# Token projections, gates and branch products of a hybrid attention block: fp16 halves scaled by powers of two in place of fp32r halves

## The chip, the cores and the metric

The kernel runs on one core of a Trainium2 chip. A core has a matrix engine (PE, with its weight loads shown apart as PEld), a vector engine (DVE), a scalar engine (ACT), a general engine (POOL) and a queue that issues DMAs (SP). Matmuls write to PSUM, an accumulator memory in banks of 512 fp32 columns; everything else lies in SBUF, 128 partitions wide. The metric is the device time of one execution in microseconds, the median of several runs.

## The reference

One decoder layer over 528 tokens (16 learned meta tokens and 512 real ones) with a model width of 1024. Two attention branches of 16 heads each, MLA and a forgetting attention (FoX), run on the same normalized input `u`; one projection `w_in` gives all branch inputs and gates:

```python
u = rmsnorm(h, pre_norm_g[l])
proj = u @ w_in[l]
(cq, ckv, k_pe_raw, z_mla, fq, fk, fv, f_logit, z_fox, gate_a, gate_b) = jnp.split(proj, split_idx, axis=-1)
...
y_mla = (o_mla * jax.nn.silu(z_mla)) @ w_br_mla[l]
...
y_fox = (o_fox * jax.nn.silu(z_fox)) @ w_br_fox[l]
mixed = (jax.nn.sigmoid(gate_a) * y_mla + jax.nn.sigmoid(gate_b) * y_fox) @ w_out[l]
h = h + rmsnorm(mixed, post_norm_g[l])
```

`o_mla` and `o_fox` are causal softmax attention; FoX adds a cumulative log forget gate to its logits. All inputs are fp32.

## The kernel before, in words

Every large product is made from halves. An fp32 operand is written as `hi + lo`, where `hi` is the operand rounded to the matmul's type and `lo` the remainder, and three matmuls `hi*hi`, `hi*lo`, `lo*hi` are added in PSUM (function `unit`, lines 161 to 184). Before the change the type is fp32r everywhere but for the attention probabilities and values, which are fp16 already.

**Front** (lines 247 to 398). `front(t)` normalizes one of five token tiles (four of 128, one of 16 meta tokens), transposes it by PE into PSUM (`pt`) and writes both halves of `u` into `uTh` and `uTl`. `back(t)` makes the small projections (`psm`: the latents, the rotary key, the forget logits) from them. The queries and keys of the first FoX head pair are projected in between, and the first forget-gate sums are made.

**Attention** (lines 413 to 740). Sixteen stages: for each of 8 head pairs first FoX (`br` 1), then MLA (`br` 0). Here the order of the PE work is written out by hand. A stage issues scores (`st`), the values of the stage before (`ov`), more scores, and then a list of filling steps (`fill`): the projections that the next stage needs and the two `z` gates of the pair. A FoX stage is filled with `z` of both branches, `mq`, `mk` and the MLA `v`; an MLA stage with `fq`, `fk` and the FoX `v`. One step is three matmuls for one of the `nk` blocks of 128 rows; a unit has 8 such blocks (512 columns) or 16 (272 and then 256 columns). The softmax runs as DVE mask and minimum (line 620), ACT exponential (628), ACT and DVE making the two halves of the probabilities (655, 656), POOL the part of the meta tokens (642 to 647) and DMA transposes issued from SP (661).

**Weights.** `wload` (94) issues the DMA of a weight block of 128 x 1024 fp32 into a ring of three buffers (`wraw`); `wsplit` (112) makes its halves: a cast on ACT (line 116) and a subtraction on POOL (line 117, recorded at the helper's line 92), in rings of three. `ahead` (692) makes each unit, when it starts, issue the loads of the next three. Other engines' orders come from a planner that goes by program order, with some parts raised.

**Merge** (lines 743 to 778). The 16 blocks of the gated branch outputs `gT` are split into `gh` and `gl` (ACT line 752, DVE line 753). For each of 8 blocks of 128 output columns there are two branch products `py` (FoX first), their gated sum `tb`, its halves `mh` and `ml`, and, for the first six, two gate units (`pg`). The last product (`po`, lines 781 to 840) and the second norm follow.

Unit outputs accumulate in a ring of three PSUM banks (`acc`, 156). All matmuls go through the helper at line 86, all transposes through the one at line 89, and all low halves made by a subtraction through the one at line 92; the profile shows these lines, and the tile names tell them apart.

Of the kernel before, what the change touches and what calls it, by code (L numbers as in the profile page):

```python
# [22 lines left out]
D = 1024  # L23
# [31 lines left out]
def block_kernel(ctx: ExitStack, tc: tile.TileContext, x, meta_tokens, pre_norm_g, w_in, fox_forget_b,  # L55
# [19 lines left out]
    uTh, uTl = (const.tile([128, KD, ROW + L - META], F32R, tag=n, name=n)[:, :, ROW - META :] for n in ("uTh", "uTl"))  # L75
# [6 lines left out]
    wp = ctx.enter_context(tc.tile_pool(name="wp", bufs=3))  # L82
    uid = [0]

# [9 lines left out]
    def wload(srcs):  # L94
# [3 lines left out]
        raw = wp.tile([128, 1024], F32, tag="wraw", name=f"wraw{u}")  # L98
# [13 lines left out]
    def wsplit(ld, keep=None):  # L112

        u, raw, parts, n = ld
        wh, wl = ((keep or wp).tile([128, 1024], F32R, tag=t, name=f"{t}{u}") for t in ("wh", "wl"))
        nc.scalar.copy(wh[:, :n], raw[:, :n])  # L116
        split_lo(nc.gpsimd, wl[:, :n], raw[:, :n], wh[:, :n])
        return [(wh[:, o : o + w], wl[:, o : o + w]) for o, w in parts]

    def wunit(srcs, keep=None):  # L120
        return wsplit(wload(srcs), keep)

    def weights(srcs, wrap):

        st = {}

        def load():
            if "l" not in st:
                st["l"] = wload(srcs())

        def get():
            load()
            return wrap(wsplit(st["l"]))
        get.load = load
        return get
# [62 lines left out]
    def win_w(off, i):  # L198
        return weights(lambda: [win[:, :, off + 128 * i : off + 128 * i + 128]], lambda w: by_k(w[0], KD))
# [18 lines left out]
    def hl_done(key, n, w):  # L218

        def done(i, ps):  # L220
# [5 lines left out]

            with tc.high_priority(offset=30):
                nc.scalar.copy(hl[:, 0, o : o + w_], ps)
                split_lo(nc.vector, hl[:, 1, o : o + w_], ps, hl[:, 0, o : o + w_])
        return done  # L230

    def q_fox(pr):
        return unit(f"fq{pr}", win_w(O_FQ, pr), u_act, KD, REAL, hl_done(("q", 1, pr), S, S))

    def k_fox(pr):
        halves = hl_done(("k", 1, pr), L, HALF)
# [6 lines left out]
        return unit(f"fk{pr}", win_w(O_FK, pr), u_act, KD, ALLT, done)  # L243

    lctx = ExitStack()
    with ExitStack() as ph:
# [8 lines left out]
        hts = {}  # L257
        halves = (slice(0, 512), slice(512, D))

        def load_h(t):  # L260

            pool, tag = (wp, "wraw") if t < 3 else (pa, "ht")
            hts[t] = pool.tile([128, D], F32, tag=tag, name=f"ht{t}")
# [24 lines left out]
        for t in (4, 2, 3):  # L288
            load_h(t)
        gq = pa1.tile([128, R_Q + R_KV], F32, tag="gq", name="gq")  # L290
# [15 lines left out]
        def front(t):  # L306
# [17 lines left out]
            for sl in parts:  # L324
                nc.vector.scalar_tensor_tensor(out=hn[:rows, sl], in0=ht[:rows, sl], scalar=st1[:rows, 1:2],
                                               in1=gb[:rows, sl], op0=ALU.mult, op1=ALU.mult)
            for half in range(2):
# [4 lines left out]
                dh = uTh[:, 4 * half : 4 * half + 4, d0 : d0 + rows]  # L332
                dl = uTl[:, 4 * half : 4 * half + 4, d0 : d0 + rows]
                nc.scalar.copy(dh, pt[:, :, :rows])
                split_lo(nc.vector, dl, pt[:, :, :rows], dh)

        def back(t):
# [3 lines left out]
            passes(psm[:, q0:], lambda k: uTh[:, k, d0 : d0 + 128], lambda k: uTl[:, k, d0 : d0 + 128],  # L341
# [31 lines left out]
        qk = q_fox(0) + k_fox(0)  # L373
        for f, t in ((front, 0), (front, 1), (back, 0), (front, 4), (front, 2), (back, 1), (front, 3), (back, 2)):
            f(t)
        run(qk[:3])
# [19 lines left out]
        for i in range(2):  # L396
            nc.sync.dma_start(c_dram[i], f32(ch[:, i]))
        run(qk[7:])

    gctx = ExitStack()  # L400
    gates = [(i, br) for i in range(KD) for br in range(2)]

    def gate_unit():

        i, br = gates.pop(0)

        def done(_, ps):
            ths[i, br] = thp.tile([128, S], F32, tag="th", name=f"th{i}{br}")
            nc.scalar.activation(ths[i, br], ps, AF.Tanh, scale=0.5)
        return unit(f"pg{i}{br}", win_w((O_GA, O_GB)[br], i), u_act, KD, REAL, done)  # L410


    with ExitStack() as att:
# [99 lines left out]
        def v_unit(br, pr):  # L513
# [6 lines left out]
            else:  # L520
                get, nk, act = win_w(O_FV, pr), KD, u_act
# [362 lines left out]
```

## Time and profile before

| what | value |
|---|---|
| median of 3 runs | 632.88 us (632.61 to 634.49) |
| profiled execution, first to last instruction | 630.9 us |
| busy PE / PEld / DVE / ACT / POOL | 608.6 / 515.7 / 315.0 / 342.9 / 263.3 us |
| matmuls | 3890, each with a weight load |
| mean granted PE clock | 0.996 of full |
| front until the first FoX `v` | 0 to 58 us |
| attention, from the second stage on | 101 to 426 us, a period of two stages 43.4 us |
| merge, from the first `py` | 429 to 582 us |
| last product and second norm | 582 to 631 us |

The profile gives the profiled execution no time beside its span. Times of the stretches are read from the chain of work that ended last. "Busy" is the union of the instructions' times; matmuls overlap in it, since a matmul's record runs until its last result is out. A row of instruction groups reads: line, engine, operation, output and inputs by tile name, their shapes and types, the count; then busy us, mean ns of one, and the idle time of the engine just before them with what ended it.

### The profile page before, as it was taken

The numbers are of one execution on the slowest core, as the hardware profiler recorded it, in microseconds if no ns is written. First come the engines' busy times: TensorE is split into PE (matmuls) and PEld (weight loads), VectorE is DVE, ScalarE is ACT, GpSimd is POOL, SyncE is SP. The second block draws the span as 40 slices with busy tenths as digits, with TensorE's granted clock in tenths as the row PEclk, the third lists the DMA queues.
The fourth block names the chain that finished last, engine by engine and source line by source line (L and its number), as shares of the span: only waits on it lengthen the run. The fifth ranks groups of instructions, "written<-read, shape, count | busy, mean of one in ns | idle before, by whom it ended". The sixth has DMA issues, their size and how long they took to land.

```text
span 630.9 us, 11084 instructions
## 1 busy us (share of the span) xinstructions
PE 608.6 (96%) x3890; PEld 515.7 (82%) x3890; DVE 315.0 (50%) x883; ACT 342.9 (54%) x774; POOL 263.3 (42%) x266
## 2 busy tenths in 40 slices
PE   3999989999999999999999999999999999999996
PEld 2879767988988889889889888878888888888885
DVE  3757557467476565674673765648222022113134
ACT  5656478378477575774784776757322232232321
POOL 3224633734344353343343443542544444444620
PEclk9999989999999999999999999999999999999999
DMA  8442657856656577467467665761532333333702
GB/s 284 123 84 54 138 147 188 205 143 153 168 135 137 145 148 163 113 162 174 101 157 175 116 153 149 158 166 38 162 93 80 97 99 100 101 100 113 255 34 100
DMA packets 204864, 85.38 MB, mean 135 GB/s; under 512 B 122684, under 2 KB 197820, under 8 KB 204808
## 3 DMA queue, kind: packets, MB, share of 16 engines
q1 hardware_dynamic: 204808, 84.67, 53.0%
q8 instruction: 30, 0.49, 0.3%
q14 instruction: 26, 0.21, 0.1%
HBM read 55.21 MB, written 4.26 MB: 94 GB/s over the span
## 4 chain that ended last, share of the span: by engine, by line
PE 89%; ACT 3%; DMA 3%; DVE 1%; issue 1%; POOL 1%; SPq 1%; DVEq 0%; POOLq 0%; ACTq 0%
PE py L86 14%; PE pg L86 14%; PE z L86 12%; PE v L86 8%; PE fk L86 7%; PE st L86 7%; PE po L86 7%; PE fq L86 7%; PE ov L86 5%; PE psm L86 3%; DMA pt<-pn 2%; PE mq L86 2%; PE mk L86 1%; PE vt L89 1%; DMA wsr<-in_w_in_dram 1%
## 5 line engine op out<-in xcount | busy, mean ns | idle before, releaser
L92 POOL TENSOR_TENSOR wl<-wraw,wh 128x1024 fp32r<-128x1024 f32 (+1 forms) x90 | 207.4, 2307 | 241.4 <-ACT wh L116 232.4
L116 ACT CAST wh<-wraw 128x1024 fp32r<-128x1024 f32 (+1 forms) x90 | 89.8, 1000 | 178.8 <-issue 84.1
L628 ACT ACTIVATE sf<-sf,nb 128x144 f32<-128x144 f32 (+3 forms) x128 | 71.9, 565 | 4.1 <-DVE nb L620 4.1
L655 ACT ACTIVATE pn<-sf,ri 128x128 f16<-128x128 f32 (+3 forms) x128 | 61.5, 551 | 15.0 <-ACT sf L628 14.8
L656 DVE SCALAR_TENSOR_TENSOR pn<-sf,ri,pn 128x128 f16<-128x128 f32 (+3 forms) x128 | 65.7, 553 | 7.9 <-ACT pn L655 7.9
L767 DVE SCALAR_TENSOR_TENSOR tb<-th,py 128x512 f32<-128x512 f32 x16 | 11.0, 686 | 107.4 <-PE py L86 107.4
L86 PE MATMUL z<-uTh,wh 128*128 128x512 f32 x128 | 51.4, 401 | 0.0
L86 PE MATMUL z<-uTh,wl 128*128 128x512 f32 x128 | 50.6, 395 | 0.0
L86 PE MATMUL z<-uTl,wh 128*128 128x512 f32 x128 | 50.4, 394 | 0.0
L86 PE MATMUL pg<-uTh,wh 128*128 128x512 f32 x128 | 50.1, 392 | 0.0
L86 PE MATMUL pg<-uTl,wh 128*128 128x512 f32 x128 | 49.8, 389 | 0.0
L86 PE MATMUL pg<-uTh,wl 128*128 128x512 f32 x128 | 49.8, 389 | 0.0
L86 PE MATMUL py<-gh,wh 128*128 128x512 f32 x128 | 49.8, 389 | 0.0
L86 PE MATMUL py<-gl,wh 128*128 128x512 f32 x128 | 49.8, 389 | 0.0
L86 PE MATMUL py<-gh,wl 128*128 128x512 f32 x128 | 49.8, 389 | 0.0
L620 DVE CUSTOM_DVE_ANT_0 sf<-st,maskt 128x272 f32<-128x272 f32 (+2 forms) x128 | 48.5, 435 | 0.0
L86 PE MATMUL st<-hlk,hlq 64*128 64x272 f32 (+3 forms) x480 | 48.0, 307 | 0.4 <-DVE nb L620 0.2
L642 POOL TENSOR_TENSOR mt<-sf,ri 128x96 f32<-128x96 f32 (+1 forms) x32 | 9.5, 297 | 83.7 <-DVE ri L637 62.1
L86 PEld LDWEIGHTS st<-hlk,hlq 64*128 64x128 f32 x480 | 35.4, 185 | 6.7 <-ACT wh L116 2.5
L86 PE MATMUL fk<-uTl,wh 128*128 128x256 f32 (+1 forms) x128 | 36.6, 286 | 0.0
L86 PE MATMUL fk<-uTh,wh 128*128 128x256 f32 (+1 forms) x128 | 36.5, 285 | 0.0
L86 PE MATMUL v<-uTh,wh 128*128 128x256 f32 (+1 forms) x128 | 36.5, 285 | 0.0
(186 smaller groups left out, 1449.4 us busy)
## 6 DMA issues: line engine op xcount, KB each, us to landing
wraw<-in_w_in_dram SPq DMA_DIRECT2D x56, 512.0 KB, 3.9
wraw<-in_w_br_fox_dram SPq DMA_DIRECT2D x8, 512.0 KB, 3.6
wraw<-in_w_br_mla_dram SPq DMA_DIRECT2D x8, 512.0 KB
wraw<-in_w_out_dram SPq DMA_DIRECT2D x8, 512.0 KB, 4.5
qpe_dram<-gT SPq DMA_DIRECT2D x8, 256.0 KB
QP<-qpe_dram SPq DMA_DIRECT2D x8, 256.0 KB, 2.8
pt<-pn SPq DMA_TRANSPOSE x128, 2.5
xr<-in_x_dram SPq DMA_DIRECT2D x4, 512.0 KB
```

Source lines behind the costliest of these rows:

```text
L86: nc.tensor.matmul(*a, **k)
L89: nc.tensor.transpose(*a)
L92: eng.tensor_tensor(out=lo, in0=src, in1=f32(hi), op=ALU.subtract)
L116: nc.scalar.copy(wh[:, :n], raw[:, :n])
L620: nc.vector.tensor_tensor_reduce(out=sf_of(h, b)[:, c0 : c0 + w], in0=ps[h][:, o : o + w], in1=maskt[:, m0 : m0 + w], scale=-scale, scalar ...
L628: nc.scalar.activation(sf, sf, AF.Exp, bias=sums["nb"][:, h, b : b + 1], scale=-1.0, accum_out=sums["su"][:, h, b : b + 1])
L642: nc.gpsimd.tensor_tensor(out=mt, in0=src, in1=ri.unsqueeze(3).broadcast_to([128, 2, nb_, META]), op=ALU.mult)
L655: nc.scalar.activation(hi, sf, AF.Copy, scale=rib)
L656: nc.vector.scalar_tensor_tensor(out=lo, in0=sf, scalar=rib, in1=hi, op0=ALU.mult, op1=ALU.subtract)
L767: nc.vector.scalar_tensor_tensor(out=tb[br], in0=ths[i, br], scalar=1.0, in1=py, op0=ALU.add, op1=ALU.mult)
```

## The change

The token projections that read `u` as a whole (`fq`, `fk`, FoX `v`, `z`, the gates `pg`) and the branch products `py` take fp16 halves in place of fp32r halves. fp16 has a narrow range of exponents, so each operand is first multiplied by a power of two that is computed on the chip:

- For `u` the scale `su` comes from the largest pre-norm gain. Each token tile gets both kinds of halves: fp32r ones per tile (`uts`), read by `back`, and fp16 ones in `uTh`, `uTl`.
- For weights the scale comes from a bound on the sum of squares: ACT squares a block as soon as it is loaded (`squares`), one PE matmul against a matrix of ones (`ALL1`) sums over partitions for a batch of 2 to 4 blocks, and DVE makes the power of two and its inverse (`pow2_scale`). The high half is then made on POOL, the low half on DVE (`weights16`).
- For the branch outputs ACT squares each `gT` block when it is made, and two such matmuls in the merge give the scales of `gh` and `gl`.
- The inverse scales go into operations that read the products: the evictions of q and k, the scale of the values, the `tanh` of the gates, `z`'s factor (one small POOL operation more a stage), and, in the merge, a ratio per block between the two branches.

A batch's matmul and DVE steps stand at 3/5 of the filling of the stage before its use, in the merge one step ahead. Rings grow: `wraw` from 3 buffers to 6, the halves from 3 to 4, loads are issued four units ahead. MLA's own weights, the rotary query, the small projections and the last product keep fp32r halves; the first half of the last product's weights gets a ring of its own (`wq`).

```diff
-    uTh, uTl = (const.tile([128, KD, ROW + L - META], F32R, tag=n, name=n)[:, :, ROW - META :] for n in ("uTh", "uTl"))
+    uTh, uTl = (const.tile([128, KD, ROW + L - META], F16, tag=n, name=n)[:, :, ROW - META :] for n in ("uTh", "uTl"))
...
+    def sumsq(src, jk, acc):
+        with nc.allow_low_precision(reason="a bound for a power of two"):
+            nc.scalar.activation(jk, src, AF.Square, accum_out=acc)
...
+    def pow2_scale(s, inv, sq):
+        nc.vector.tensor_scalar(out=inv.bitcast(I32), in0=sq.bitcast(I32), scalar1=0x7F000000, scalar2=1,
+                                op0=ALU.bitwise_and, op1=ALU.logical_shift_right)
+        nc.vector.tensor_scalar(out=inv, in0=inv, scalar1=2.0 ** 50, scalar2=2.0 ** -60, op0=ALU.mult, op1=ALU.max)
+        nc.vector.reciprocal(s, inv)
...
+        def scale(self):
+            for load in self.loads:
+                load()
+            n = len(self.loads)
+            ps = acc(f"sc{self.name}")[:, :n]
+            mm(ps, ALL1, self.ssq[:, :n], start=True, stop=True)
+            sc = self.sc = wp.tile([128, 4, 4], F32, tag="sc", name=f"wsc{self.name}", bufs=8)
+            with tc.high_priority(offset=60):
+                pow2_scale(sc[:, 0, :n], sc[:, 1, :n], ps)
...
+    def weights16(src, batch):
...
+        def load():
+            if "l" not in st:
+                st["l"] = wload([src()])
+                batch.squares(j, st["l"][1])
+        def get():
+            u, raw, _, n = st["l"]
+            wh, wl = (wp.tile([128, n], F16, tag=t, name=f"{t}{u}") for t in ("wh", "wl"))
+            s = batch.col(0, j)
+            nc.gpsimd.tensor_scalar(out=wh, in0=raw, scalar1=s, scalar2=None, op0=ALU.mult)
+            nc.vector.scalar_tensor_tensor(out=wl, in0=raw, scalar=s, in1=wh, op0=ALU.mult, op1=ALU.subtract)
...
+                dh, dl = (u[:, hs, :rows] for u in uts[t])
+                nc.scalar.copy(dh, src)
+                split_lo(nc.vector, dl, src, dh)
+                dh, dl = (u[:, hs, d0 : d0 + rows] for u in (uTh, uTl))
+                nc.scalar.activation(dh, src, AF.Copy, scale=su)
+                nc.vector.scalar_tensor_tensor(out=dl, in0=src, scalar=su, in1=dh, op0=ALU.mult, op1=ALU.subtract)
...
+        first[-2:-2] = [(100, batches[0].scale)]
+        for fill, batch in zip(fills, batches[1:]):
+            n = len(fill) * 3 // 5
+            fill[n:n] = [(100, batch.scale)]
...
         for br in (1, 0):
+            ps = acc(f"gs{br}")[:, 0:KD]
+            mm(ps, ALL1, gss[:, br, 0:KD], start=True, stop=True)
+            nc.vector.tensor_reduce(out=sg[br], in_=ps, op=ALU.add, axis=AX.X)
+            pow2_scale(sg[br], isg[br], sg[br])
...
             for k in range(KD):
-                nc.scalar.copy(gh[br][:, k], gT[br][:, k])
-                split_lo(nc.vector, gl[br][:, k], gT[br][:, k], gh[br][:, k])
+                hi, lo, g = (t[br][:, k] for t in (gh, gl, gT))
+                nc.scalar.activation(hi, g, AF.Copy, scale=sg[br])
+                nc.vector.scalar_tensor_tensor(out=lo, in0=g, scalar=sg[br], in1=hi, op0=ALU.mult, op1=ALU.subtract)
...
+        merge[0][2].scale()
+        for e, (t, x, batch) in enumerate(merge):
+            if e + 1 < len(merge):
+                merge[e + 1][2].scale()
```

More of the change, by code (lines that the diff above doesn't have):

```diff
@@ L97, in wload @@
         u = uid[0]
-        raw = wp.tile([128, 1024], F32, tag="wraw", name=f"wraw{u}")
+        raw = wp.tile([128, 1024], F32, tag="wraw", name=f"wraw{u}", bufs=6)
         n = 0
@@ L242, in done, with gate_w @@
                     nc.sync.dma_start(f32(CT[64 * h : 64 * h + 2, :]), c_dram[:, 2 * pr + h, :])
-        return unit(f"fk{pr}", win_w(O_FK, pr), u_act, KD, ALLT, done)
+        return unit(f"fk{pr}", w, u_act, KD, ALLT, done)
+    gates = [(i, br) for i in range(KD) for br in range(2)]
+    def gate_w(batch):
+        i, br = gates.pop(0)
+        w = win_w((O_GA, O_GB)[br], i, batch)
+        w.gate = i, br
+        return w
     lctx = ExitStack()
@@ L711, in block_kernel @@
             else:
-                g = gate_unit()
-                fill = g[:4] + vts[br, pr] + g[4:] + gate_unit()
+                g, g2, g3 = (gate_unit(gate_w(batch)) for _ in range(3))
+                fill = g[:4] + vts[br, pr] + g[4:] + g2
+                tail = g3
             if si == 0:
@@ L758, in block_kernel @@
         ml = mp.tile([128, KD, S], F32R, tag="ml", name="ml")
-        for i in range(KD):
+        merge[0][2].scale()
+        for e, (t, x, batch) in enumerate(merge):
+            if e + 1 < len(merge):
+                merge[e + 1][2].scale()
+            for _, _, late in merge[e + 2 : e + 3]:
+                for load in late.loads:
+                    load()
+            if t == "g":
+                for w in x:
+                    run(gate_unit(w))
+                continue
+            i = x
             tb = {}
-            for br in (1, 0):
-                def get(br=br):
-                    return by_k(wunit([wbr[br][:, :, 128 * i : 128 * i + 128]])[0], KD)
+            for br, w in zip((1, 0), batch.w):
                 def done(_, py, br=br):
```

200 lines of the change are left out of this document (140 added, 60 removed).

## The prediction

> **What bounds the kernel now.** I read the page first (busy shares, then the chain of work that ended last), next the same chain in order of time, then the busy times by stretch.
>
> ```profile
> span 630.9 us, 11084 instructions
> PE 608.6 (96%) x3890; PEld 515.7 (82%) x3890; DVE 315.0 (50%) x883; ACT 342.9 (54%) x774; POOL 263.3 (42%) x266
> ...
> PE 89%; ACT 3%; DMA 3%; DVE 1%; issue 1%; POOL 1%; SPq 1%; DVEq 0%; POOLq 0%; ACTq 0%
> ```
>
> ```profile
> 242.32 5.83 PE fk L86 x48
> ...
> 266.62 2.74 PE z L86 x12
> ...
> 275.98 1.97 PE ov L86 x26
> ...
> 429.24 10.88 PE py L86 x48
> 440.12 10.88 PE pg L86 x48
> ```
>
> ```profile
> 14.00:28.00 14.00, 14.00 (x73) 12.87 (x73) 11.19 (x22) 8.39 (x24) 3.01 (x1) 1.00 0.48 151
> 28.00:41.00 13.00, 11.43 (x60) 8.90 (x59) 8.49 (x26) 9.13 (x28) 7.12 (x3) 1.00 0.66 139
> ...
> 232.00:275.00 43.00, 43.00 (x336) 37.13 (x334) 26.50 (x90) 28.72 (x72) 17.18 (x25) 1.00 0.66 151
> ...
> 473.00:560.00 87.00, 87.00 (x385) 72.06 (x385) 16.74 (x16) 23.24 (x29) 39.56 (x16) 1.00 0.34 96
> ```
>
> The columns of the last fence are the stretch, its length, then busy us of PE, weight load, DVE, ACT, POOL, the granted clock and DMA. PE carries 89% of the chain, and from about 100 us on it never rests; so a matmul that starts its successor sooner shortens the span, and anything PE has to wait for lengthens it. At 429 us a matmul of 512 columns takes 10.88/48 = 227 ns, though its row says 389 (pipelined): I cost matmuls by start to start. At 242 us one pair of `fk` (272 and 256 columns) takes 5.83/24 = 243 ns. DVE and ACT rest about a third of an attention period (43 us) but have little rest in 14 to 41 us.
>
> **The matmuls.** 2112 change type: `z`, `pg`, `py` 384 each and `fq` 192 with 512 columns, `fk` and the FoX `v` 384 each in pairs of 272 and 256. The trace has fp16 matmuls only in the attention values:
>
> ```profile
> 256.05 1.80 PE L86 MATMUL ov<-pt,vp 128*64 128x512 f16 x24
> ```
>
> ```profile
> L86 PE MATMUL ov<-pt,vp 128*64 128x512 f16 x96 | 13.7, 380 | 0.0
> ...
> L86 PE MATMUL ov<-pt,vp 128*64 128x128 f16 x96 | 5.9, 219 | 0.0
> L86 PEld LDWEIGHTS <-vp 128*64 128x64 f16 x384 | 21.2, 110 | 8.4
> L86 PEld LDWEIGHTS py<-gh,wh 128*128 128x128 f32 x128 | 24.0, 188 | 5.0
> ```
>
> Those 24 are twelve pairs (two heads side by side) of 3840 columns together. A column costs (380 - 219)/384 = 0.419 ns. From the first start to the last the block takes 1.80 - 0.22 = 1.58 us for eleven pairs of 3712 columns, which need 1.555; 25 ns are left, 2 per pair. Of the fp32r matmul's 227 ns, 512 columns leave 12.5. So I take 217 ns for 512 columns in fp16 and 528 x 0.419 + 4 = 225 for a pair of 272 and 256: 1344 x 10 + 384 x 18 = **-20.4 us**. Both ends: 0 if the 12.5 ns belong to swapping 128 weight columns (these rows swap 64), -25 if nothing is left over. I take the rows' value: two weight sets per pair are swapped there for 2 ns.
>
> **Small matmuls added.** Each batch of weights sums its squares over partitions by one matmul against all-ones: 2 batches in front, 16 in the stages, 14 in the merge, and 2 for the branch outputs: 34. Nearest row, four transposes of 128 columns with a weight load each:
>
> ```profile
> 151.29 0.44 PE vt L89 x4
> ```
>
> 110 ns each: **+3.7 us** (0 if they vanish in the stream; a wait comes on top, below).
>
> **Weights.** The halves change engine: ACT squares instead of casting, POOL makes the scaled high half, DVE the low half, for 72 of 90 weights.
>
> ```profile
> L92 POOL TENSOR_TENSOR wl<-wraw,wh 128x1024 fp32r<-128x1024 f32 x80 | 194.3, 2432 | 217.9 <-ACT wh L116 212.6 <-DMA pt<-pn 3.5 <-PE po L86 1.8
> L116 ACT CAST wh<-wraw 128x1024 fp32r<-128x1024 f32 x80 | 83.6, 1048 | 159.7 <-issue 82.6 <-PE py L86 33.9 <-PE pg L86 17.6
> L322 ACT ACTIVATE hn<-ht 128x1024 f32<-128x1024 f32 x3 | 3.2, 1060 | 0.0
> L628 ACT ACTIVATION_READ_ACCUMULATOR sf<-sf,nb 128x1 f32 x128 | 24.1, 188 | 0.0
> L325 DVE SCALAR_TENSOR_TENSOR hn<-ht,st,gb 128x1024 f32<-128x1024 f32 x3 | 3.8, 1279 | 0.0
> L645 POOL CAST pn<-mt 128x96 f16<-128x96 f32 x16 | 4.6, 287 | 1.1
> L645 POOL CAST pn<-mt 128x32 f16<-128x32 f32 x16 | 3.4, 212 | 1.0
> L536 DVE RECIPROCAL vsc<-vsc 128x1 f32<-128x1 f32 x16 | 2.6, 164 | 0.6
> ```
>
> Per weight: ACT 1.06 + 0.19 instead of 1.05; DVE +1.28; POOL between the casts' slope (75 ns for 64 columns, so 1.4 us for 1024) and 2.43; I take 1.4, since it has one tensor input like the casts. Each batch adds five DVE operations of 0.16 us. Per attention period (five weights, two batches) DVE gets 8.0 us, POOL loses 5. DVE's 16.5 us of rest hide that by throughput, and in the merge (16.7 busy of 87) all of it. POOL's gain is worth nothing: PE does not wait for it. The scaled q/k evictions and the merge's extra scalings keep the length of what they replace.
>
> **A wait added in the FoX stages.** The batch matmul stands at 3/5 of the fill, two steps into the second `z` unit, and takes one of three accumulator banks. One bank holds that unit, one `mq`, and the third is free only when DVE has read the first `z`:
>
> ```profile
> 267.31 0.69 DVE L573 SCALAR_TENSOR_TENSOR sil<-sil,z 128x512 f32<-128x512 f32 x1 [0.62 <-ACT sil L572]
> ```
>
> It ends at 268.00. PE gets there at 266.62 + 2 x 0.684 = 267.99 now, and 0.3 us sooner with shorter matmuls (30 x 10 ns); behind it wait the rest of `z`, `mk` and `v`, since PE runs in order. About 0.3 us in each of 8 stages: **+2.4 us**. Low end 0. High end: if each of five low halves waited out a POOL operation of 2.43, DVE's 8.0 + 12.2 would pass its 16.5 - 1.6 of rest by 5.3 us a period, 42 us.
>
> **The front.** Every token tile now gets two sets of halves: fp32r for the small projection, fp16 for the rest.
>
> ```profile
> L92 DVE TENSOR_TENSOR uTl<-pt,uTh 128x512 fp32r<-128x512 f32 x8 | 5.2, 683 | 1.5 <-ACT uTh L334 1.5
> L334 ACT CAST uTh<-pt 128x512 fp32r<-128x512 f32 x8 | 4.4, 589 | 4.6 <-PE pt L89 4.6
> L528 DVE TENSOR_REDUCE vsc<-v 128x1 f32<-128x272 f32 x16 | 7.0, 440 | 19.8 <-PE v L86 19.8
> ```
>
> DVE: 8 x 0.68 + 0.4, the gain's maximum (440 ns for 272 columns, so 1.2 for 1024) with three small steps 1.7, two low halves 2.6, a batch 0.8: 11 us, against 2.8 + 4.5 of rest in 14 to 41 us. ACT: 5.1 + four squares 5.0 - three casts 3.1, within its 9.5. So DVE spills 11.0 - 7.3 = **+3.7 us** (0 if the order lets it slip past 41 us; 11 if none hides).
>
> **The start of the merge.** Now the halves of `gT` run just ahead of the first `py`:
>
> ```profile
> 427.96 9.88 DVE L92 TENSOR_TENSOR gl<-gT,gh 128x512 fp32r<-128x512 f32 x16 [0.81 <-ACT gh L752]
> ```
>
> ```profile
> L752 ACT CAST gh<-gT 128x512 fp32r<-128x512 f32 x16 | 8.5, 621 | 4.3 <-DVE gT L676 4.3
> ```
>
> The last low half ends at 437.84; the eighth step of the second `py` unit needs it at 440.12 - 0.68 = 439.44, so 1.6 us ahead, 1.1 with a PE 0.5 us quicker. After the change the scale's matmul stands behind the last gate unit (429.24); four small DVE operations, a high half and the signals between put the first low half at 430.9, 2.9 later. DVE also gets a second scale (0.7), the batch's six small steps (1.0) and two low weight halves (2.6) in this row. 2.9 - 1.1 + 4.3 = **+6.1 us**; low end 1.8 if the 4.3 goes elsewhere, high end 11 if both low weight halves wait for POOL (2 x 2.43).
>
> **Sum.** -20.4 + 3.7 + 2.4 + 3.7 + 6.1 = -4.5 us: a span of 626.4. The profiled span (630.9) is 2.0 below the runs' median (632.88), so I forecast 628.4.
>
> **A rule against the change.** The trace has the same subtraction twice, without POOL beside it (`gl`, 685 ns) and with:
>
> ```profile
> L92 DVE TENSOR_TENSOR gl<-gT,gh 128x512 fp32r<-128x512 f32 x16 | 9.8, 685 | 0.9 <-ACT gh L752 0.8
> L92 DVE TENSOR_TENSOR ml<-tb,mh 128x512 fp32r<-128x512 f32 x8 | 16.9, 2112 | 5.5 <-ACT mh L771 5.5
> ```
>
> The Trainium skill, "SBUF — State Buffer", section "Who interferes with whom", says that a DVE instruction with two SBUF inputs and a GpSimd instruction that reads SBUF exclude one another for the whole instruction. The trace agrees (2112 against 685 ns). The new low weight halves are such instructions and the new high halves such POOL work; that is the second rival.
>
> **Rivals.** (1) *The cover holds everywhere*: no spill in front, no wait in the stages, 1.8 at the merge. -20.4 + 3.7 + 1.8 = -14.9: 618.0. For it: the rest in the windows; against: PE's place in order behind `gT`'s scale.
>
> (2) *Slower: low weight halves fall into the FoX stage's chain from scores to probabilities.* Its transposes go out here:
>
> ```profile
> 261.21 1.18 SPq L661 DMA_TRANSPOSE pt<-pn  x1
> ...
> 264.71 7.96 SPq L661 DMA_TRANSPOSE pt<-pn  x6
> ```
>
> ```profile
> pt<-pn SPq DMA_TRANSPOSE x128, 2.5
> ```
>
> The queue is full from 261.21 to 272.67, each issue taking some 1.3 us; the last lands 2.5 after its issue, about 273.9, and PE wants it at 275.98: 2.0 us ahead, 1.5 with shorter matmuls. If both `z` weights' low halves run in the DVE work before it, each with half a POOL operation (0.7) of waiting, the chain is 2 x 1.98 late, 2.5 us over the slack in 8 stages, 19.7 instead of 2.4: 645.7. The kernel turns slower once a stage loses 0.9 us, that is from 2.4 us of delay. Against it: DVE's rest.
>
> (3) *No change*: only the merge start at its high end, 11 for 6.1: 633.3.
>
> (4) *It doesn't do what it says*: 128-column fp16 weights are spaced like fp32r. Without the first term the rest is +15.9: 648.8. Against it: the 2 ns above.
>
> **Chances.** Forecast 0.44, rivals 0.17, 0.20, 0.13, 0.06. Its own range is 623 to 632; to hold 8 in 10 I reach to 616 and, into the second rival, 641. A difference of 0.3% (1.9 us, the spread of the three runs) is what can be told from none. Faster: the first rival and 0.40 of the forecast, 0.57. Same: 0.17, the third and the forecast's rest. Slower: 0.26.
>
> **What would show it.** 48 matmuls of `py` or `pg` in 10.4 us instead of 10.88, a pair of `fk` in 225 ns: right on the first term; unchanged: rival 4. A gap of PE at the first `py` near 6 us; a wait of the batch matmul for `sil`; `fq` 3 to 4 us later in front; `ml`-like lengths (over 2 us) of DVE's low weight halves inside the FoX stages with PE waiting for `pt` would be rival 2. The forecast is wrong if a wait outside these places costs PE more than 5 us.

## The result and the profile after

The changed kernel takes 778.24 us (median of 4 runs, 777.18 to 780.18) where the kernel before takes 632.99 (4 runs): a ratio of 1.2285, 95% interval 1.2243 to 1.2328. That is 145 us slower; the forecast was 628.4, and its range ended at 641.

The head of the page of the changed kernel (its line numbers are higher than those of before, by 9 and more: matmuls L95, subtractions L101, squares L92, high weight halves L204, low ones L205):

```profile
span 776.5 us, 11481 instructions
PE 641.3 (83%) x3924; PEld 393.9 (51%) x3924; DVE 466.2 (60%) x1153; ACT 369.0 (48%) x888; POOL 312.8 (40%) x291
```

PE was busy 96% of the span and is busy 83% now: it doesn't work for 135 us where it rested 22. It is also busy 33 us longer, although fp16 matmuls in a running stream start closer together (e1, below). The busy times by stretch show where (columns as in the prediction: stretch, length, PE, weight load, DVE, ACT, POOL, granted clock, DMA share and GB/s):

```profile
0.00:62.00 62.00, 43.66 (x229) 33.64 (x229) 38.43 (x98) 39.72 (x102) 15.61 (x20) 0.97 0.51 138
62.00:110.00 48.00, 33.70 (x208) 21.65 (x208) 33.30 (x74) 26.36 (x58) 26.45 (x31) 0.93 0.52 117
110.00:560.00 450.00, 367.48 (x2583) 234.03 (x2584) 280.76 (x787) 237.53 (x615) 168.93 (x205) 0.92 0.53 113
560.00:579.00 19.00, 9.49 (x35) 3.42 (x34) 18.40 (x39) 11.85 (x19) 14.17 (x4) 0.73 0.11 28
579.00:777.00 198.00, 186.96 (x873) 101.21 (x871) 95.27 (x158) 53.48 (x95) 87.60 (x32) 0.97 0.34 101
```

From 110 to 560 us, in the attention stages, PE rests 83 of 450 us, and the granted clock falls to 0.92. After a rest, matmuls of 512 columns start 0.43 us apart for a while, and only then 0.22; here behind a wait of 3.62 us for `sil` (start, us, engine, instruction; in brackets the idle time ahead and what ended it):

```profile
346.64 0.17 PE L95 MATMUL scs<-ssqs,ALL 128*128 128x3 bf16 x1 [3.62 <-DVE sil L683]
...
347.39 0.63 PE L95 MATMUL z<-uTh,wl 128*128 128x512 f16 x1
347.82 0.63 PE L95 MATMUL z<-uTh,wh 128*128 128x512 f16 x1
...
351.21 0.38 PE L95 MATMUL z<-uTl,wh 128*128 128x512 f16 x1
351.43 0.38 PE L95 MATMUL z<-uTh,wl 128*128 128x512 f16 x1
```

No other engine is full either: DVE is busy 62% of that stretch. So this is not an engine that ran out of time, but a chain of waits.

The costliest groups for the weights, and the waits of the whole run that bear on them (engine, line, what it waited for, total us, times, longest):

```profile
L204 POOL TENSOR_SCALAR wh<-wraw,wscs 128x1024 f16<-128x1024 f32 x40 | 116.3, 2915 | 90.8 <-DVE wscs L181 77.1
L205 DVE SCALAR_TENSOR_TENSOR wl<-wraw,wscs,wh 128x1024 f16<-128x1024 f32 x40 | 74.2, 1854 | 62.2 <-POOL wh L204 62.1
L92 ACT ACTIVATE jks<-wraw 128x1024 bf16<-128x1024 f32 x40 | 42.1, 1053 | 78.7 <-DMA wraw<-in_w_in_dram 78.5
```

```profile
DVE wl L205 <- POOL wh L204: 96.4, 58, 2.8
ACT jks L92 <- DMA wraw<-in_w_in_dram: 78.5, 19, 11.9
POOL wh L204 <- DVE wscs L181: 77.1, 15, 7.7
SPq L116 <- DVE wl L205: 177.8, 35, 23.7
PE st L95 <- DVE nb L730: 25.2, 25, 7.3
PE scs L95 <- DVE sil L683: 22.9, 7, 3.6
PE v L95 <- DVE hlk L101: 19.6, 8, 3.9
```

Together they form a chain. The batch's scale releases POOL's high half (2.9 us each); DVE's low half waits for it (58 times); a loaded buffer is free only when its low half is made, and SP's next weight load waits for that; ACT's square, standing in ACT's order, waits for the load to land (up to 11.9 us), with the exponentials of the softmax behind it. The batch matmul reads the squares, but in the stages it waited for one only once (1.8 us), and seven times for `sil`. Four waits from 110 to 560 us alone:

```profile
SPq L116 <- POOL wl L101: 41.0, 7, 7.5
SPq L116 <- DVE wl L205: 26.0, 8, 3.7
PE st L95 <- DVE nb L730: 17.9, 24, 2.0
PE vt L98 <- DVE nb L730: 15.3, 8, 3.6
```

So most of SP's 177.8 us lie outside the stages. Inside them the loads wait longer for POOL's low halves of MLA's fp32r weights, which stand in POOL's order behind the multiplications. And PE's rest of 83 us is nearly all in waits for DVE: 33.2 us for the masks (`nb`), 22.9 for `sil`, 19.6 for the low halves of the keys (`hlk`), beside 6.4 for ACT's squares of `gT`. One pass through the chain, from the timeline:

```profile
319.24 0.17 PE L95 MATMUL scs<-ssqs,ALL 128*128 128x2 bf16 x1
319.27 0.27 PE L95 MATMUL fk<-uTh,wh 128*128 128x256 f16 x1
320.21 5.72 POOL L204 TENSOR_SCALAR wh<-wraw,wscs 128x1024 f16<-128x1024 f32 x2 [6.86 <-DVE wscs L181]
323.13 2.14 DVE L205 SCALAR_TENSOR_TENSOR wl<-wraw,wscs,wh 128x1024 f16<-128x1024 f32 x1 [2.34 <-POOL wh L204]
325.90 1.29 POOL L101 TENSOR_TENSOR wl<-wraw,wh 128x512 fp32r<-128x512 f32 x1
325.96 2.31 DVE L205 SCALAR_TENSOR_TENSOR wl<-wraw,wscs,wh 128x1024 f16<-128x1024 f32 x1 [0.69 <-POOL wh L204]
327.21 0.37 SPq L116 DMA_DIRECT2D wraw<-in_w_in_dram  x1
332.39 1.06 ACT L92 ACTIVATE jks<-wraw 128x1024 bf16<-128x1024 f32 x1 [11.62 <-DMA wraw<-in_w_in_dram]
338.93 0.17 DVE L746 TENSOR_SCALAR su<-su 128x6 f32<-128x6 f32 x1 [6.34 <-ACT sf L738]
```

The load at 327.21 has waited 6.5 us for POOL's fp32r low half, which ends at 327.19, behind the two multiplications. ACT stands for 11.62 us until 332.39 for a load, and the sums of the softmax (`su`), which wait for the exponentials, begin at 338.93, 12.0 us after the stage's attention values (326.96). The batch matmul itself costs PE nothing that can be seen: its neighbour starts 0.03 us later.

At the merge, PE has to wait three times more:

```profile
560.21 0.19 PE L95 MATMUL gs<-gss,ALL 128*128 128x8 bf16 x2
561.65 6.79 POOL L204 TENSOR_SCALAR wh<-wraw,wscy 128x1024 f16<-128x1024 f32 x2 [13.76 <-DVE wscy L181]
564.57 0.39 PE L95 MATMUL py<-gh,wh 128*128 128x512 f16 x1 [3.62 <-POOL wh L204]
570.11 0.59 PE L95 MATMUL py<-gh,wh 128*128 128x512 f16 x1 [4.93 <-ACT gh L897]
571.27 0.61 PE L95 MATMUL py<-gh,wl 128*128 128x512 f16 x1 [0.56 <-DVE wl L205]
571.67 0.63 PE L95 MATMUL py<-gh,wh 128*128 128x512 f16 x1
572.09 0.63 PE L95 MATMUL py<-gl,wh 128*128 128x512 f16 x1
...
576.36 0.38 PE L95 MATMUL py<-gl,wh 128*128 128x512 f16 x1
576.58 0.38 PE L95 MATMUL py<-gh,wl 128*128 128x512 f16 x1
```

PE waits 3.62 us for a high half from POOL, 4.93 for a high half of `gT` from ACT and 0.56 for a low half from DVE. Then the starts are 0.42 us apart, and only from about 575 us on 0.22. The Trainium skill, "TensorE: Matmul & The Clock Gate", section "Wait — 56ns, not 53.3ns?", gives 426.7 ns for 512 columns on a cold array and 215.7 on a warm one; this trace agrees with both.

### The profile page after: what moved, and what is told of

It is laid out like the page before. It is cut to its first block, busy times and chain, and to the rows that moved or that the text cites. A ratio compares the mean times of both kernels' runs of the same rounds, so it can differ in the third digit from the quotient of the medians.

```text
span 776.5 us, 11481 instructions
## 1 busy us (share of the span) xinstructions
PE 641.3 (83%) x3924; PEld 393.9 (51%) x3924; DVE 466.2 (60%) x1153; ACT 369.0 (48%) x888; POOL 312.8 (40%) x291
## 5 line engine op out<-in xcount | busy, mean ns | idle before, releaser
L95 PEld LDWEIGHTS <-wh 128*128 128x128 f16 x1408 | 136.7, 101 | 154.6 <-issue 51.5
L204 POOL TENSOR_SCALAR wh<-wraw,wscs 128x1024 f16<-128x1024 f32 x40 | 116.3, 2915 | 90.8 <-DVE wscs L181 77.1
L205 DVE SCALAR_TENSOR_TENSOR wl<-wraw,wscs,wh 128x1024 f16<-128x1024 f32 x40 | 74.2, 1854 | 62.2 <-POOL wh L204 62.1
L95 PEld LDWEIGHTS <-wl 128*128 128x128 f16 x704 | 71.2, 101 | 68.8 <-issue 13.5
L95 PE MATMUL st<-hlk,hlq 64*128 64x272 f32 (+3 forms) x480 | 59.1, 325 | 26.3 <-DVE nb L730 25.2
L92 ACT ACTIVATE jks<-wraw 128x1024 bf16<-128x1024 f32 x40 | 42.1, 1053 | 78.7 <-DMA wraw<-in_w_in_dram 78.5
L204 POOL TENSOR_SCALAR wh<-wraw,wscy 128x1024 f16<-128x1024 f32 x16 | 46.9, 2942 | 48.7 <-DVE wscy L181 48.7
L95 PEld LDWEIGHTS st<-hlk,hlq 64*128 64x128 f32 x480 | 41.5, 192 | 40.6 <-DVE nb L730 33.9
L95 PE MATMUL py<-gh,wh 128*128 128x512 f16 x128 | 50.6, 395 | 11.6 <-POOL wh L204 6.7
L95 PE MATMUL z<-uTh,wh 128*128 128x512 f16 x128 | 56.0, 437 | 0.0
L95 PE MATMUL z<-uTh,wl 128*128 128x512 f16 x128 | 54.8, 428 | 0.0
L95 PE MATMUL z<-uTl,wh 128*128 128x512 f16 x128 | 54.7, 428 | 0.0
L95 PE MATMUL py<-gh,wl 128*128 128x512 f16 x128 | 50.7, 396 | 2.2 <-DVE wl L205 2.1
L95 PE MATMUL py<-gl,wh 128*128 128x512 f16 x128 | 50.3, 393 | 0.0
L95 PE MATMUL pg<-uTh,wh 128*128 128x512 f16 x128 | 48.5, 379 | 0.1
L95 PE MATMUL pg<-uTh,wl 128*128 128x512 f16 x128 | 48.5, 379 | 0.0
L95 PE MATMUL pg<-uTl,wh 128*128 128x512 f16 x128 | 48.5, 379 | 0.0
```

Source lines behind the costliest of these rows:

```text
L92: nc.scalar.activation(jk, src, AF.Square, accum_out=acc)
L95: nc.tensor.matmul(*a, **k)
L204: nc.gpsimd.tensor_scalar(out=wh, in0=raw, scalar1=s, scalar2=None, op0=ALU.mult)
L205: nc.vector.scalar_tensor_tensor(out=wl, in0=raw, scalar=s, in1=wh, op0=ALU.mult, op1=ALU.subtract)
```

## The experiments

To compare places as well as totals, I divide each profiled span at the first attention values (`ov`) of the first and of the last stage: front, stages, merge with the last product. The kernel before has 98.0, 326.2 and 206.6 us, the changed kernel 117.5, 436.9 and 222.1.

The experiments make a ladder from the types alone to the whole change; the table is the summary, the texts follow. "Kernel before" stood at 631.6 to 634.3 us in these comparisons.

| kernel | us | ratio to before, 95% | front | stages | merge |
|---|---|---|---|---|---|
| e1 fp16 types alone | 612.88 | 0.9663 (0.9627 to 0.9700) | 95.9 | 316.6 | 199.7 |
| e7 and scales of u and gT, weights split as before | 626.01 | 0.9878 (0.9838 to 0.9918) | 101.2 | 316.7 | 206.6 |
| e6 and low halves on DVE, a fixed scale | 641.56 | 1.0124 (1.0090 to 1.0158) | 101.4 | 330.7 | 205.9 |
| e2 and high halves on POOL | 693.42 | 1.0945 (1.0890 to 1.1000) | 101.4 | 381.2 | 207.4 |
| e3 and squares on ACT, unused | 740.65 | 1.1691 (1.1629 to 1.1752) | 110.4 | 420.0 | 210.2 |
| e11 and batch matmuls and scale steps, unused | 735.29 | 1.1604 (1.1572 to 1.1636) | 107.7 | 415.2 | 210.2 |
| the change: scales used | 778.24 | 1.2285 (1.2243 to 1.2328) | 117.5 | 436.9 | 222.1 |

Up to e11 the weights' scale doesn't come from the data: e1 has no scales at all, the others a constant for the weights and scales from the data for `u` and `gT`. So none of them guards weights of an unusual size as the change does.

**e1: the types alone.** The kernel before, its tiles made fp16, the halves made on ACT and POOL as before. The small projections (`psm`) take fp16 halves here too, which the change keeps in fp32r: 120 matmuls, some 1 us by an estimate of 10 ns each.

```diff
-    uTh, uTl = (const.tile([128, KD, ROW + L - META], F32R, tag=n, name=n)[:, :, ROW - META :] for n in ("uTh", "uTl"))
+    uTh, uTl = (const.tile([128, KD, ROW + L - META], F16, tag=n, name=n)[:, :, ROW - META :] for n in ("uTh", "uTl"))
...
-            return wrap(wsplit(st["l"]))
+            return wrap(wsplit(st["l"], None, dt))
```

> The kernel before with fp16 in place of fp32r for the halves of u, of the weights that meet u, of the branch outputs and of their weights, with no scales, no squares and the halves made where they were (ACT and POOL). It measures the first term of the prediction alone. If the matmuls' spacing is all that fp16 changes: 630.9 - 20 = 611 in the span, 613 as a time. If fp16 matmuls themselves bring waits (their weight loads are instructions of their own), it stays above 640.

Measured: 612.88 us. Two rows of its chain of waits, in order of time (start, us, matmuls):

```profile
362.96 5.40 PE fk L86 x48
417.82 10.36 PE py L86 x48
```

48 matmuls of 512 columns in 10.36 us are 216 ns each, a pair of 272 and 256 columns 5.40/24 = 225 ns. The span is 18.6 us below the one before (612.3 against 630.9). The first term of the prediction holds, and this kernel beats both.

**e12: the types alone with deeper rings** (4 weight buffers and pairs of halves in place of 3, loads one unit earlier).

```diff
-    wp = ctx.enter_context(tc.tile_pool(name="wp", bufs=3))
+    wp = ctx.enter_context(tc.tile_pool(name="wp", bufs=4))
...
-                fn.nxt = [f.load for f in fns[n + 1 : n + 4]]
+                fn.nxt = [f.load for f in fns[n + 1 : n + 5]]
```

> The kernel with only the types changed (612.9 us), with a ring of 4 in place of 3 weight buffers and pairs of halves (the fp16 tiles make room) and loads issued 4 units ahead in place of 3. Theory D (with the conversions on ScalarE and GpSimd everything is covered; TensorE is busy 95% of the span): 608 to 614 us, no gain beyond the uncertainty. The rival (some of the 27 us in which TensorE isn't busy are late weights): 600 to 606 us.

Measured: 614.92 us (ratio 0.9691, 0.9657 to 0.9724), the same as e1 within the uncertainty. With the conversions on ACT and POOL, weights are not what PE waits for.

**e2 and e3: fixed scales, without and with the squares.** e2 uses 1024 for every weight and leaves out squares, batch matmuls and scale steps; e3 keeps the squares on ACT, which nobody reads.

```diff
-                batch.squares(j, st["l"][1])
...
-            return self.sc[:, i, j : j + 1]
+            return yfix[:, i, j : j + 1] if self.other else wfix[:, i : i + 1]
```

> The changed kernel with a constant scale of 1024 for all weights: no squares of weights, no batch matmul, no DVE steps for a scale; the high halves stay on POOL, the low halves on DVE, the scales of u and of the branch outputs stay as they are. Theory Q (the softmax is late because the squares stand in front of it in ACT's queue and wait there for weight loads, which wait for buffers that are freed only after the batch matmul): the period of two stages falls from 59 to about 45 us, the time to 640 to 660. Theory P (the conversions' own price, POOL 2.9 us and DVE 2.1 us with the port taken): the period stays above 54, the time above 735.

> As the kernel with constant scales, but ACT still squares each weight block when it is loaded, with nothing reading the sums. Buffers are then freed early, so weight loads come early. Theory Q in its two parts: if the squares' 1.25 us each in front of the softmax is what costs, 680 to 720; if it is their wait for late loads, little above the kernel without squares (within 10 us). Theory P: the same as the kernel without squares, both above 735.

Measured: 693.42 and 740.65 us. Neither theory had e2: with no chain through a scale at all, 80 us over e1 stay. The squares add 47. Waits of e2:

```profile
DVE wl L194 <- POOL wh L193: 111.5, 53, 7.6
PE st L99 <- DVE nb L721: 31.3, 29, 5.4
```

DVE, which works in order, stands at a low half until POOL has made the high half, and the masks (`nb`) behind it come late for the scores. This became the new theory (D in the expectations below), and the next runs test it.

**e4: squares later**, just ahead of the batch matmul in place of right after the load.

```diff
             n = len(self.loads)
+            for j in range(n):
+                self.squares(j, self.raws[j])
             ps = acc(f"sc{self.name}")[:, :n]
```

> The changed kernel with the squares of a batch issued just ahead of its matmul and not at the load, so that they stand behind the stage's exponentials and not in front of them; all else, scales from the data included, as in the changed kernel. Theory Q: the softmax is on time again, the period falls to about 50 us (the batch matmul now waits up to 3 us for its squares), the time to 690 to 715. Theory P: no gain, 770 or more.

Measured: 774.34 us (1.2222, 1.2165 to 1.2280). That is the outcome that theory P named. The place in ACT's queue is worth some 4 us, if anything (the intervals overlap): at the later place the loads are still not there (ACT waits 76.6 us for them, against 78.5).

**e5, e6, e7: which engine makes the halves.** e5 puts the high half on POOL as a plain conversion and the low half on DVE in e1; e6 moves e2's high half to ACT; e7 gives e2 both engines of the kernel before (a weight scale of 1).

```diff
 # e5, in e1
+            nc.gpsimd.tensor_copy(wh[:, :n], raw[:, :n])
+            split_lo(nc.vector, wl[:, :n], raw[:, :n], wh[:, :n])
 # e6, in e2
-            nc.gpsimd.tensor_scalar(out=wh, in0=raw, scalar1=s, scalar2=None, op0=ALU.mult)
+            nc.scalar.activation(wh, raw, AF.Copy, scale=s)
 # e7, in e2
+            nc.scalar.copy(wh, raw)
+            split_lo(nc.gpsimd, wl, raw, wh)
```

> The kernel with only the types changed (612.9 us, conversions on ScalarE and GpSimd as before), and of the change one part more: the high half of every fp16 weight made on GpSimd (a plain conversion), the low half on VectorE (a subtraction), with no scale, no squares, no batch matmul, one pair of u halves. Theory D (VectorE executes in order and stands at the low half until GpSimd has made the high half of 2.9 us; the masks and the softmax steps stand behind it): two stages go from 42.2 to some 50 us, as in the kernel with fixed scales (51.5), so 8 x 8 to 9 us more and some at the merge: 670 to 695 us. Theory F (the swap is harmless; the 80 us of the kernel with fixed scales come from its second pair of u halves, its scaled evictions and its later start of the merge): within 10 us of 612.9, 605 to 625 us.

> The kernel with fixed scales (693.4 us), the high half moved from GpSimd to ScalarE, the low half left on VectorE. Theory D: the low half no longer waits 2.9 us for GpSimd, and the two engines no longer share the port for it; VectorE still has 1.3 us per weight more than before. Two stages go from 51.5 to 43 to 46 us: 625 to 655 us. Theory F (VectorE's own load of low halves, or the front, the evictions and the merge, cost the 80 us): 680 us or more.

> The kernel with fixed scales (693.4 us) with a scale of 1 for the weights, so that ScalarE can make the high half and GpSimd the low half by a subtraction, as in the kernel before; u and the branch products keep their scales from the data, so the front, the scaled evictions and the scales' work at the merge stay. Theory D: what is left over the 612.9 us of the kernel with only the types changed is the second pair of u halves in front (its first FoX batch starts about 6 us later in the kernel with fixed scales) and the later merge (13 us from the last branch products to the first output of the merge): 620 to 640 us. Theory F: 670 us or more.

Measured: e5 654.12 us (1.0319, 1.0278 to 1.0360), e6 641.56, e7 626.01. Theory F falls with all three; theory D's sizes hold for e6 and e7, but e5, whose swap is the same, costs 41 us where D said 57 to 82. A row that I hadn't known when I wrote the expectation says why it is less:

```profile
L117 POOL CAST wh<-wraw x72: 1033/1042/4470, 19.4 to 583.9; 128x1024 f16<-128x1024 f32 x72
```

A plain conversion on POOL takes 1.04 us (shortest, median and longest stand after the count), not the 2.9 of the multiplication. e7 also shows 5.3 us over e1 in the front, where the second pair of `u` halves is made, and 6.9 in the merge with its scales, and that the scaled evictions cost nothing: its stages take 316.7 us, e1's 316.6.

**e13 and e14: POOL's length, or POOL's place.** Both are e2 with a weight scale of 1. e13 makes the high half on POOL as a conversion, the low half on DVE; e14 keeps POOL's long multiplication and puts the low half on POOL too.

```diff
 # e13
-            nc.gpsimd.tensor_scalar(out=wh, in0=raw, scalar1=s, scalar2=None, op0=ALU.mult)
-            nc.vector.scalar_tensor_tensor(out=wl, in0=raw, scalar=s, in1=wh, op0=ALU.mult, op1=ALU.subtract)
+            nc.gpsimd.tensor_copy(wh, raw)
+            split_lo(nc.vector, wl, raw, wh)
 # e14
+            nc.gpsimd.tensor_scalar(out=wh, in0=raw, scalar1=batch.col(0, j), scalar2=None, op0=ALU.mult)
+            split_lo(nc.gpsimd, wl, raw, wh)
```

> The kernel with fixed scales (693.4 us) with a weight scale of 1, the high half still on GpSimd but as a plain conversion (1.04 us in the kernel with swapped engines) in place of the multiplication by a scale (2.85 us), the low half on VectorE by a subtraction of its usual 1.27 us. With the high half on ScalarE it took 641.6 us, so GpSimd costs 52 us. Theory L (the length of GpSimd's operation, 1.8 us more per weight, is what VectorE's queue stands for): 645 to 660 us. Theory Q (GpSimd's queue is the wrong place at any length, since the conversion stands there until TensorE frees a pair of halves, with the softmax's GpSimd steps behind it): 675 us or more.

> The kernel with fixed scales (693.4 us) with a weight scale of 1; the high half stays a multiplication on GpSimd (2.85 us) and the low half moves there too (a subtraction, some 2.1 us), so VectorE has none of it and ScalarE neither. With both halves on the engines of before it took 626.0 us. Theory V (what costs is VectorE standing, in order, for GpSimd's high half, the masks behind it): GpSimd is busy some 5 us for each of 72 weights, 360 of 626 us, and VectorE free: 625 to 645 us. Theory G (what costs is GpSimd itself: its part of the softmax stands behind 2.85 us conversions, and the two engines share the port): 690 us or more.

Measured: e13 641.28 us (1.0149, 1.0120 to 1.0179), e14 637.15 (1.0080, 1.0057 to 1.0103). Theories Q and G fall; e14 lies in theory V's range, e13 4 us below theory L's. The waits of e13 that answer to those of e2, and POOL's row of e14:

```profile
DVE wl L105 <- POOL wh L193: 40.8, 32, 4.0
PE st L99 <- DVE nb L721: 2.6, 2, 2.4
```

```profile
L193 POOL TENSOR_SCALAR wh<-wraw,wfix 128x1024 f16<-128x1024 f32 x56 | 164.3, 2934 | 30.9 <-PE fk L99 11.2
```

With a short conversion POOL is as good a place as ACT (641.28 against e6's 641.56). And with both halves on POOL its multiplications are as long as in e2, but the stages take 320.8 us in place of 381.2. So neither POOL's load nor its place costs the 52 us between e6 and e2: the pair does, DVE's low half behind a long POOL operation.

The swap of engines has no fixed price: with plain conversions it costs 15 us in e13 (against e7) and 41 in e5 (against e1). e13 has the change's longer rings (six loaded blocks, four pairs of halves, loads four units ahead), e5 has rings of three. That the rings make the difference was not tried.

**e8: the whole change with the high half on ACT**, scales from the data kept (the edit of e6).

> The changed kernel (778.2 us), the high half moved from GpSimd to ScalarE; the squares, the batch matmuls and the scales from the data stay. Theory D with the squares as a second cost in the same chain: GpSimd's 2.9 us leave the chain from the batch matmul to the freed weight buffer, and the squares wait less for late loads: 690 to 730 us. The rival (what costs is the batch matmul's place and the loads behind it, whoever converts; ScalarE, which carries the squares already, gets another 1.1 us per weight): 765 us or more.

Measured: 719.33 us (1.1354, 1.1315 to 1.1393), as theory D said. 59 us of the change's loss go with POOL's multiplication, the rest stays.

**e9 and e10: why the squares cost.** e9 squares 128 of 1024 columns of a weight; e10 has eight weight buffers for six and loads issued 6 units ahead. To make room in e10, the squares of the branch outputs share a scratch tile with those of the weights, and `wq` has three pairs in place of four.

```diff
 # e9
-            sumsq(raw, jk, self.ssq[:, j : j + 1])
+            sumsq(raw[:, 0:128], jk[:, 0:128], self.ssq[:, j : j + 1])
 # e10
-        raw = wp.tile([128, 1024], F32, tag="wraw", name=f"wraw{u}", bufs=6)
+        raw = wp.tile([128, 1024], F32, tag="wraw", name=f"wraw{u}", bufs=8)
...
-                fn.nxt = [f.load for f in fns[n + 1 : n + 5]]
+                fn.nxt = [f.load for f in fns[n + 1 : n + 7]]
```

> The changed kernel (778.2 us); the squares are taken over the first 128 columns of each weight tile alone, at the same places in ScalarE's queue (the scales are then a bound for an eighth of the weights). An estimate for such a square from the 1.06 us of 1024 columns and the 0.6 us of 512: 0.2 to 0.3 us, so 0.8 us less for each of 72. Theory B (the squares cost by their own time on ScalarE, ahead of the exponentials; the step with the squares unused was 47 us): 735 to 750 us. Theory W (they cost by standing in ScalarE's queue until a late load lands, 11.9 us at the longest, whatever their length): 765 us or more.

> The changed kernel (778.2 us) with 8 buffers for the loaded weights in place of 6 and loads issued 6 units ahead in place of 4; to make room, the squares of the branch products share a scratch tile with those of the weights, and 3 in place of 4 pairs of halves serve the first half of the output projection. Theory W (the squares wait for loads that are issued late because a buffer is freed late): with two more buffers the loads start before the low halves are done, ScalarE's waits for weight loads (78.5 us for the stages and some 45 at the merge) mostly go: 735 to 755 us. Theory B (the squares' own time on ScalarE): 770 to 785 us.

Measured: e9 757.17 us (1.1932, 1.1895 to 1.1969), e10 747.67 (1.1795, 1.1759 to 1.1831). The group of squares in the stages, first e9, then e10 (busy, mean ns | idle ahead):

```profile
L92 ACT ACTIVATE jks<-wraw 128x128 bf16<-128x128 f32 x40 | 12.2, 305 | 81.4 <-DMA wraw<-in_w_in_dram 81.3
```

```profile
L92 ACT ACTIVATE jks<-wraw 128x1024 bf16<-128x1024 f32 x40 | 41.8, 1045 | 0.2
```

In e9 a square takes 0.31 in place of 1.05 us and waits as long as ever: 21 us are gained, between the two theories. In e10 the waits are gone from the stages, 31 us are gained, and the time lies in theory W's range. So both count, the squares' own time and their wait, and by these two runs the wait is the larger one.

**e11: scales taken but not used.** The edit of `col` in e2, with squares, batch matmuls and scale steps all kept.

> The changed kernel (778.2 us) with squares, batch matmuls and VectorE's scale steps all kept, but the conversions and evictions use the fixed scale 1024. The kernel that also leaves out the batch matmuls and scale steps took 740.7 us. Theory C (the 38 us between them are the chain from batch matmul over the scale to the conversion: the halves are late, so the buffers are): 738 to 750 us. Theory S (they are the queue slots: TensorE stands at the batch matmul for an accumulator bank and VectorE at the scale steps for the matmul, whoever uses the result): 765 to 785 us.

Measured: 735.29 us, no more than e3 (740.65) and 3 below theory C's range. The queue slots of 34 matmuls and their DVE steps cost nothing; using their result costs 43 us (778.24 - 735.29). Why is argued, not shown. Theory C's reason, late buffers, doesn't fit ACT's waits for the stages' weights: they are 100.9 us in e11 and 78.5 in the change. What grows are PE's waits for work that stands in DVE's order: for the keys' low halves (`hlk`) from 2.6 to 20.0 us, for `sil` from 11.7 to 22.9; 14.0 us for the scale steps themselves (`wscs`, at `mk`) in e11 are gone.

## Why the prediction was wrong, by its own steps

**Right, and of the right size.** The matmuls: 217 and 225 ns were said, 216 and 225 measured; -20.4 us against 18.6 between the spans. The front, +3.7 said, is 5.3 in e7, and the merge's start, +6.1 said, is 6.9 there. e7, which has the types, the second pair of `u` halves and the merge's scales but none of the weights' new work, takes 626.0. Without its terms for the batch matmuls and for `sil` (6.1 us), my sum is 622.3: it was in effect a forecast for this kernel. In the whole change both places cost more, 21.6 and 22.4 us over e1. By the table that comes with the squares (9.0 in front and 2.8 in the merge, e3 against e2) and with the use of the scales (9.8 and 11.9, the change against e11).

**The step that failed: "DVE's 16.5 us of rest hide that by throughput".** I set the weights' new work at nothing since the engines had time. Three things went wrong in it.

- The size of POOL's high half. I had no row for a multiplication by a per-partition scale on POOL and took 1.4 us from the slope of its small casts. The cast would have been 1.04, the multiplication is 2.85 (median), above my upper bound of 2.43. With DVE behind it this is 52 us (e2 against e13). I had the mechanism on paper: the high end of my term for the FoX stages, each low half waiting out a POOL operation, is 42 us, and e2 against e6 measures 50.5 in the stages. But I left it out of the sum, and the range ended at 641.
- The order. Rest is of use only if the work may move into it. A low half stands at its place in DVE's queue, and masks and softmax sums behind it; DVE is busy only 62% of the stages and sets the pace all the same. Even without the long POOL operation the stages lose 14.0 us when DVE makes the low halves and ACT a scaled high half (e6 against e7), where I said 0.
- The buffers. I counted ACT's 1.25 us per square and looked at ACT's load alone. I didn't ask when a loaded buffer comes free now: after scale, high half and low half. Loads then start late, and the square, in order ahead of the exponentials, hands the delay to the softmax. That and the squares' own time are 47 us (e3 against e2), and the use of the scales 43 more. The late loads don't need the wait for a scale: e3 has none, and there ACT waits 102.9 us for the stages' weights.

**The small terms.** A batch matmul was put at 110 ns, 3.7 us in all; in the trace the next matmul starts 0.03 us later. The added wait for `sil` in the FoX stages was found where it was predicted, but is ten times as long (22.9 us over the run, 2.4 said); still, e11, which has 11.7 us of it, is no slower than e3, which has 3.5 at `mk`: it hides in delays that are there already.

**The rivals.** Rival 2 named the right engine and order, low halves in the DVE work of the FoX stage's chain from scores to probabilities, and the right sign, and the low halves' lengths of over 2 us came out (2.14 median). But the wait that it named, PE for the transposed probabilities `pt`, is 0.9 us in all; PE waits for masks, `sil` and `hlk`. And it priced the delay by 0.7 us of waiting per half and 8 stages: 645.7. That e6 and e13 come near to this time is no support for it, since both lack the long POOL operation. The order of ACT and the buffers stood in no rival. Rival 4 falls by e1. The condition that I had set, a wait outside the named places that costs PE more than 5 us, is met by the 25.2 us that the scores wait for masks.

**The rule.** The low weight half takes 1.85 us on average in the stages of the changed kernel and 1.29 in e6, where ACT makes the high half:

```profile
L194 DVE SCALAR_TENSOR_TENSOR wl<-wraw,wfix,wh 128x1024 f16<-128x1024 f32 x56 | 72.4, 1293 | 58.3 <-ACT wh L193 57.4
```

That is what the Trainium skill, "SBUF — State Buffer", section "Who interferes with whom", leads one to expect of a DVE instruction with two SBUF inputs beside POOL. 0.56 us for 40 halves are 22 us of DVE in the stages. Of the 52 us between e6 and e2, the lock seems the smaller part: in the stages of e2 DVE is busy 9.7 us longer (255.7 against 246.0) and stands 27.8 us longer for high halves (49.8 against 22.0). The exact shares stay open: both need the low half on DVE beside a long POOL operation, and e13 and e14 take both away at once. The softmax's own DVE work beside POOL is not it: in e14 POOL is busy longer (464 us in the run, 324 in e2) and the stages are 60 us shorter.

**What stays open.** The ladder's rungs are differences in one order; e8 against e6 puts squares and scales together at 78 us without POOL, e3 and the change against e2 at 85 with it, so the rungs depend on one another by some 7 us. How the 31 and 21 us of e10 and e9 add up was not tried together. Which link makes the use of the scales cost 43 us isn't shown either.

## What to carry to other kernels

Work moved to an engine that has rest is free only if its place in that engine's order is: before you cost it at nothing, write down what stands behind it and when its inputs are there. When a conversion gets a longer chain ahead of it (load, square, sum, scale, high half, low half), ask when its buffer is freed, what load that starts, and who stands in order behind the first reader of that load. And test the part that promises the gain alone: here the types gave 3.4%, and all the rest of the change only cost.

## What the hardware showed that I had not expected

- On POOL, fp32 to fp16 over 128 x 1024 takes 1.04 us as a conversion and 2.85 as a multiplication by a per-partition scale; on ACT the two are 1.05 and 1.15. The groups of ACT's high halves, first in e7 (conversion), then in e6 (multiplication), with busy us and mean ns behind the bar:

```profile
L193 ACT CAST wh<-wraw 128x1024 f16<-128x1024 f32 x72 | 75.1, 1045 | 120.9 <-PE v L99 40.6
```

```profile
L193 ACT ACTIVATE wh<-wraw,wfix 128x1024 f16<-128x1024 f32 x56 | 64.2, 1148 | 85.5 <-PE v L99 40.0
```

- A matmul of two columns in a running stream delays the next by only 0.03 us, weight load included (319.24 to 319.27).
- Rests of a few us on PE cost twice: the rest itself, and then half speed (starts 0.43 us apart in place of 0.22 after the wait of 3.62 us at 346.64). In the changed kernel PE is busy 641.3 us, in e1, with 34 matmuls fewer, 584.7.
